# Latent attention in fp32 on one core: fixed places in the issue order for the probability splits, the output weights and the late loads

## The chip, the cores and the metric

The kernel runs on one of the eight cores of a Trainium2 chip. A core has a matrix engine (PE, whose weight loads are listed as PEld), a vector engine (DVE), an activation engine (ACT), a general engine (POOL), and a queue engine (SP) that issues most of the transfers. Each engine works through its own list of instructions in a fixed order, and waits on semaphores where it needs another engine's result. The metric is the device time of one execution in microseconds. Before the change it is 598.81 us, the median of three runs (596.79 to 600.26).

## The reference

The model has one layer that is used: an RMS norm, multi-head latent attention with a SiLU gate, an output projection, a residual add, and a last RMS norm. The sequence has 1024 positions, the width is 1024, there are 8 heads, everything is float32. Cut to what matters:

```
proj = rms_norm(x) @ w_in                     # c_q (384), c_kv (256), k_pe (64), gate (1024)
q = (rms_norm(c_q) @ w_uq)                    # 8 heads x (128 + 64 rotary)
k_nope, v = split(rms_norm(c_kv) @ w_ukv)     # 8 heads x (128, 128)
s = q_nope @ k_nope.T + rope(q_pe) @ rope(k_pe).T
p = softmax(s * scale)                        # per head, 1024 x 1024
o = (p @ v) * silu(gate)
y = rms_norm(x + o @ w_out)
```

## The kernel before

Float32 products are made of three products in a faster format: each operand is split into a high part and a low part (`hi` is a cast, `lo` is the operand less `hi`), and `mm3` issues high by high, high by low and low by high. So each operand of a product costs a cast, usually on ACT or POOL, and a subtraction, on DVE or POOL.

The program has three stages. In the first, up to about 175 us, the input projection, the gates, the norms and the rotary parts are made. In the second, 175 to 490 us, attention runs over 64 blocks: block u is head u // 8 and query rows (u % 8) * 128 to + 127. In the third the output projection runs over 8 row tiles and two column halves.

A block goes through this chain. `scores` (line 451) issues ten matmuls of 512 columns into a PSUM tile `s`; there are two such tiles, so block u + 2 can only start when block u has been read. DVE takes the row maxima (`nmx`, line 464). ACT takes the exponential into the tile `probs` with the row sums `sm` (line 466). DVE makes the reciprocal `rc` (line 471), POOL multiplies by it (line 472), and DVE transposes within 32 by 32 squares (line 473). Four blocks make a group g and share one `probs` tile, of which there are two. After the fourth, `exchange` (line 475) finishes the transpose across partitions by 16 transfers on SP from `probs` to a tile `d`. `split_part` (line 483) then splits one half of `d`, in two pieces c = 0 and 1: two casts `pt_h` on ACT (line 488), and the low parts `pt_l`, the first piece on DVE (line 490), the second half on DVE (line 492) and half on POOL (line 493). There are three buffers for the pieces. `values` (line 499) issues 12 matmuls for each half of a group, and after the second half DVE multiplies the result into `gate` (line 516). Beside that, each head makes its queries, keys and values from latent tensors (`q`, `k`, `v`), each with a cast on ACT and a subtraction on DVE.

In the last head the output weights are loaded on SP (`fetch_w_out`, line 523, four buffers `wor`) and split (`split_w_out`, line 527: a cast `woh` on ACT, a subtraction `wol` on DVE or POOL). `out_start` (line 547) loads a piece of x, splits the gated result of heads 0 to 6 into `o_split` (cast on ACT, subtraction on DVE) and issues 21 matmuls `o`; `out_end` adds head 7 and the residual.

The order in which the instructions of an engine stand is not the order in which the Python writes them. At build time a scheduler plays the program against its own expectation of durations and puts each instruction where that expectation has it ready, with the order of writing as priority (`later` moves a helper's priority back). The chip then follows that fixed order, whatever the real durations are. In the main loop (line 653) step u writes the scores of block u, and at even u the split of half `two` of group g, with u = 8 + 4 g + 2 two; at odd u the values of it.

Of the kernel before, what the change touches and what calls it, by code (L numbers as in the profile page):

```python
# [29 lines left out]
def kernel(  # L30
# [415 lines left out]
    produce_q(q_now, 0, w_q)  # L446
    produce_v(v_now, 0, w_v)

    square, part = {}, {}

    def scores(u, q, kx, qpe):
        half, qs = (u % 8) // 4, slice((u % 4) * P, (u % 4 + 1) * P)
        s = wide("s")
        qpe_s = qpe[half][:, qs]
        for kb in range(2):
            ks = halves(kb)
            mm3(s[:, ks], q[half][0][:, qs], q[half][1][:, qs], kx[kb][0], kx[kb][1], True, False)
            mm(s[:, ks], lhsT=qpe_s, rhs=kk_h[:, ks], start=False, stop=False)  # L458
            mm(s[:, ks], lhsT=qpe_s, rhs=kk_l[:, ks], start=False, stop=True)  # L459
        if u % 4 == 0:  # L460
            square[u // 4] = turned_tile("probs").rearrange("p j (k t c) -> p j k t c", k=8, t=4)
        p_t = square[u // 4][:, :, :, u % 4]
        nmx = column("nmx")
        nc.vector.tensor_reduce(nmx, s, axis=AX.X, op=ALU.max, negate=True)  # L464
        sm = column("sm")
        nc.scalar.activation(  # L466
            p_t.rearrange("p j k c -> p k j c"), s.rearrange("p (k j c) -> p k j c", k=8, j=4),
            AF.Exp, bias=nmx, accum_out=sm,
        )
        rc = column("rc")  # L470
        nc.vector.reciprocal(rc, sm)  # L471
        nc.gpsimd.tensor_scalar(p_t, p_t, rc, 1.0, op0=ALU.mult, op1=ALU.mult)  # L472
        nc.vector.transpose(out=p_t, in_=p_t)  # L473

    def exchange(g):

        src = square.pop(g).rearrange("p j k t c -> p j (k t c)")
        d = part[g] = at.tile([P, 4, L], F32, name="d", tag="d")
        for a in range(4):
            for j in range(4):  # L480
                nc.sync.dma_start(d[j * 32:(j + 1) * 32, a], src[a * 32:(a + 1) * 32, j])  # L481

    def split_part(g, two):

        for c in range(2):
            src = part[g][:, :, (two * 2 + c) * 256:(two * 2 + c + 1) * 256]
            hi, lo = split_tiles("pt")
            nc.scalar.copy(hi, src)  # L488
            if c == 0:
                nc.vector.tensor_sub(lo, src, f32(hi))  # L490
            else:
                nc.vector.tensor_sub(lo[:, 0:2], src[:, 0:2], f32(hi[:, 0:2]))  # L492
                nc.gpsimd.tensor_sub(lo[:, 2:4], src[:, 2:4], f32(hi[:, 2:4]))  # L493
            split_keys.append((hi, lo))
# [158 lines left out]
    for u in range(U + 10):  # L653
# [15 lines left out]
        if u % 2 == 0 and u >= 8:  # L669
            g, two = (u - 8) // 4, (u - 8) % 4 // 2  # L670
            if g < U // 4:
                split_part(g, two)
        if u % 2 == 1 and u >= 9:
            g, two = (u - 9) // 4, (u - 9) % 4 // 2
            if g < U // 4:
# [3 lines left out]
            split_w_out(H - 2, 0)  # L679
        if u == U + 1:  # L680
            split_w_out(H - 1, 0)
            for k in range(3):
                fetch_w_out(k, 1)
            y_sb = turned_tile("y_sb").rearrange("p a b -> p (a b)")
            gf_sb = wop.tile([P, D], F32, name="gf_sb")
            nc.sync.dma_start(gf_sb, gf)
            nc.gpsimd.tensor_scalar(gf_sb, gf_sb, -0.5, 1.0, op0=ALU.mult, op1=ALU.mult)
        if u in (U + 1, U + 3):
            started.append(out_start(0, len(started)))
        if u == U + 3:  # L690
            started.append(out_start(0, 2))
            out_end(started[0])
# [14 lines left out]
                produce_v(v_now, i - 3, w_v)  # L707
        if h == H - 1:
            if i >= 2:
                split_w_out(i - 2, 0)  # L710
            if i >= 1:
                fetch_w_out(i - 1, 0)
            continue
# [78 lines left out]
```

## Time and profile before

| what | us |
|---|---|
| median of three runs | 598.81 |
| the profiled execution | 599.52 |
| its span, first to last instruction | 597.7 |
| PE busy | 575.8 |
| DVE busy | 432.4 |
| ACT busy | 276.9 |
| POOL busy | 226.0 |
| mean granted PE clock, of 1 | 0.988 |

Three things help to read it. The end of a matmul is modelled: one of 512 columns is shown as 0.39 us long, while the next one starts 0.23 us after it, so PE is shown as busy even where it is only just kept fed, and its real lost time is found from the starts. The clock column says what share of full speed PE was granted: it falls after a pause. And a wait is put down to the last event that ended it; with engines that work in fixed order, what stands in front of an instruction matters as much as what it needs.

### The profile page before, as it was taken

The page shows a single profiled execution, that of the slowest core. Times are in us where ns is not written, and L with a number is a line of the kernel's source. Part 1 is how long each engine was busy: PE and PEld are TensorE (multiplying, and loading weights), DVE is VectorE, ACT ScalarE, POOL GpSimd, SP SyncE. Part 2 cuts the span into 40 slices and gives each one's busy share as a digit, 9 for nine tenths or more (in the row PEclk, how much of TensorE's full clock was granted, in tenths as well). Part 3 has the DMA queues.
Part 4 walks back from the last instruction along what each step waited for, and adds up shares of the span by engine and source line. Part 5 has one row for each costly group of instructions (what it writes and reads, how often), then busy time and mean ns, then how long its engine had stood idle before and what let it go on. Part 6 is the DMA issues. An engine that isn't in the chain of part 4 may idle for free.

```text
span 597.7 us, 7666 instructions
## 1 busy us (share of the span) xinstructions
PE 575.8 (96%) x2604; PEld 474.9 (79%) x2604; DVE 432.4 (72%) x578; ACT 276.9 (46%) x437; POOL 226.0 (38%) x197
## 2 busy tenths in 40 slices
PE   9999999999999999999999999999699979999995
PEld 6888888888888778877888778888588758888885
DVE  6912588565237899889898988988769995784653
ACT  4357553021024456526545444646346743554652
POOL 3513502343102353454344533455242664483000
PEclk9999999999999999999999999999889999999998
DMA  8666222233211646577617467353664886231342
GB/s 299 238 207 230 88 72 64 96 106 140 89 49 35 143 111 153 138 164 163 140 41 176 110 152 167 94 115 78 142 140 106 247 212 137 93 105 54 123 141 106
DMA packets 35963, 78.66 MB, mean 132 GB/s; under 512 B 7314, under 2 KB 11154, under 8 KB 35860
## 3 DMA queue, kind: packets, MB, share of 16 engines
q1 hardware_dynamic: 34628, 76.17, 47.0%
q10 hardware_dynamic: 1296, 2.01, 0.9%
q8 instruction: 20, 0.33, 0.2%
q14 instruction: 19, 0.16, 0.1%
HBM read 36.19 MB, written 8.41 MB: 75 GB/s over the span
## 4 chain that ended last, share of the span: by engine, by line
PE 64%; SPq 12%; DVE 8%; issue 7%; DMA 4%; ACT 3%; POOL 1%; POOLq 0%; ACTq 0%; DVEq 0%
SPq L481 12%; PE g L60 6%; PE g L59 6%; PE g L61 6%; PE o L61 5%; PE o L60 5%; PE o L59 5%; DVE probs L473 3%; PE pv L59 2%; PE pv L60 2%; PE pv L61 2%; PE s L59 2%; PE s L60 2%; PE s L458 2%; PE s L61 2%
## 5 line engine op out<-in xcount | busy, mean ns | idle before, releaser
L472 POOL TENSOR_SCALAR probs<-probs,rc 128x1024 f32<-128x1024 f32 x64 | 83.5, 1306 | 112.1 <-DVE rc L471 102.1
L466 ACT ACTIVATE probs<-s,nmx 128x1024 f32<-128x1024 f32 x64 | 71.4, 1116 | 99.8 <-DVE nmx L464 94.3
L473 DVE STREAM_TRANSPOSE probs<-probs 128x1024 f32<-128x1024 f32 x64 | 78.9, 1234 | 10.5 <-POOL probs L472 9.6
L464 DVE TENSOR_REDUCE nmx<-s 128x1 f32<-128x1024 f32 x64 | 76.8, 1208 | 9.9 <-PE s L459 9.7
L488 ACT CAST pt_h<-d 128x1024 fp32r<-128x1024 f32 x64 | 65.6, 1050 | 27.4 <-DMA d<-probs 13.4
L60 PE MATMUL g<-xl,gwh 128*128 128x512 f32 x160 | 62.3, 390 | 0.0
L61 PE MATMUL g<-xh,gwl 128*128 128x512 f32 x160 | 62.3, 389 | 0.0
L59 PE MATMUL g<-xh,gwh 128*128 128x512 f32 x160 | 62.3, 389 | 0.0
L493 POOL TENSOR_TENSOR pt_l<-d,pt_h 128x512 fp32r<-128x512 f32 x32 | 48.8, 1525 | 35.4 <-ACT pt_h L488 35.1
L59 PE MATMUL s<-k_h,q_h 128*128 128x512 f32 x128 | 50.4, 396 | 6.7 <-ACT probs L466 6.7
L59 PE MATMUL pv<-pt_h,v_h 128*128 128x512 f32 x128 | 50.5, 394 | 4.7 <-ACT pt_h L488 4.7
L490 DVE TENSOR_TENSOR pt_l<-d,pt_h 128x1024 fp32r<-128x1024 f32 x32 | 42.7, 1334 | 10.9 <-ACT pt_h L488 7.5
L60 PE MATMUL pv<-pt_l,v_h 128*128 128x512 f32 x128 | 50.1, 391 | 0.5 <-POOL pt_l L493 0.4
L60 PE MATMUL s<-k_l,q_h 128*128 128x512 f32 x128 | 50.0, 390 | 0.0
L458 PE MATMUL s<-kk_h,qpe 128*128 128x512 f32 x128 | 49.9, 390 | 0.0
L61 PE MATMUL s<-k_h,q_l 128*128 128x512 f32 x128 | 49.9, 390 | 0.0
L459 PE MATMUL s<-kk_l,qpe 128*128 128x512 f32 x128 | 49.9, 390 | 0.0
L61 PE MATMUL pv<-pt_h,v_l 128*128 128x512 f32 x128 | 49.9, 390 | 0.0
L61 PE MATMUL o<-woh,o_split 128*128 128x512 f32 (+1 forms) x118 | 45.1, 386 | 2.4 <-DVE o_split L576 2.4
L60 PE MATMUL o<-wol,o_split 128*128 128x512 f32 (+1 forms) x118 | 45.2, 383 | 0.0
L59 PE MATMUL o<-woh,o_split 128*128 128x512 f32 (+1 forms) x118 | 45.0, 383 | 0.0
L492 DVE TENSOR_TENSOR pt_l<-d,pt_h 128x512 fp32r<-128x512 f32 x32 | 32.9, 1029 | 4.7 <-ACT pt_h L488 4.7
(193 smaller groups left out, 1250.2 us busy)
## 6 DMA issues: line engine op xcount, KB each, us to landing
d<-probs SPq DMA_DIRECT2D x256, 128.0 KB
gwr<-in_wg SPq DMA_DIRECT2D x20, 256.0 KB
craw_b<-in_x SPq DMA_DIRECT2D x8, 512.0 KB
qpe<-qpe_d SPq DMA_DIRECT2D x16, 256.0 KB
wor<-in_wo SPq DMA_DIRECT2D x16, 256.0 KB
xr<-in_x SPq DMA_DIRECT2D x16, 256.0 KB
xr<-in_xT SPq DMA_DIRECT2D x5, 512.0 KB
qpe_d<-craw_a SPq DMA_DIRECT2D x8, 256.0 KB
```

What stands on the lines that cost most here:

```text
L59: mm(ps, lhsT=lh, rhs=rh, start=first, stop=False)
L60: mm(ps, lhsT=lh, rhs=rl, start=False, stop=False)
L61: mm(ps, lhsT=ll, rhs=rh, start=False, stop=last)
L458: mm(s[:, ks], lhsT=qpe_s, rhs=kk_h[:, ks], start=False, stop=False)
L459: mm(s[:, ks], lhsT=qpe_s, rhs=kk_l[:, ks], start=False, stop=True)
L464: nc.vector.tensor_reduce(nmx, s, axis=AX.X, op=ALU.max, negate=True)
L466: nc.scalar.activation(p_t.rearrange("p j k c -> p k j c"), s.rearrange("p (k j c) -> p k j c", k=8, j=4), AF.Exp, bias=nmx, accum_out=sm,)
L472: nc.gpsimd.tensor_scalar(p_t, p_t, rc, 1.0, op0=ALU.mult, op1=ALU.mult)
L473: nc.vector.transpose(out=p_t, in_=p_t)
L481: nc.sync.dma_start(d[j * 32:(j + 1) * 32, a], src[a * 32:(a + 1) * 32, j])
L488: nc.scalar.copy(hi, src)
L493: nc.gpsimd.tensor_sub(lo[:, 2:4], src[:, 2:4], f32(hi[:, 2:4]))
```

## The change

`tc.issue_after(ins)` adds an edge of order to each instruction written in its block, on the engine of `ins`: it stands behind `ins` in that engine's list. It adds no semaphore. The change keeps each block's exponential in `exps[u]` and the last transfer of each exchange in `moves[g]`, and uses them in five places:

- the split of a half group, written at step u, has its casts on ACT behind the exponential of block u - 1 (the split of group g, first half, behind block 4 g + 7; second half behind block 4 g + 9);
- in the last head the split of output weight i - 2, written at step u, has its cast behind the exponential of block u - 1;
- the load of the last norm's gain `gf` and the first three loads of the second half of the output weights stand on SP behind the last transfer of the last exchange;
- the first two `out_start` have their casts on ACT behind the last exponential, and their loads of x on SP behind the last exchange;
- the weight loads are written after the load of `gf`, no longer before it.

No operation is added or removed. Since the scheduler plays the program again with these edges, the order on all engines moves after the first few blocks.

```diff
-    square, part = {}, {}
+    square, part, exps, moves = {}, {}, {}, {}
...
-        nc.scalar.activation(
+        exps[u] = nc.scalar.activation(
             p_t.rearrange("p j k c -> p k j c"), s.rearrange("p (k j c) -> p k j c", k=8, j=4),
             AF.Exp, bias=nmx, accum_out=sm,
         )
...
-                nc.sync.dma_start(d[j * 32:(j + 1) * 32, a], src[a * 32:(a + 1) * 32, j])
+                moves[g] = nc.sync.dma_start(d[j * 32:(j + 1) * 32, a], src[a * 32:(a + 1) * 32, j])
...
             if g < U // 4:
-                split_part(g, two)
+                with tc.issue_after(exps[min(u, U) - 1].ins):
+                    split_part(g, two)
...
             split_w_out(H - 1, 0)
-            for k in range(3):
-                fetch_w_out(k, 1)
             y_sb = turned_tile("y_sb").rearrange("p a b -> p (a b)")
             gf_sb = wop.tile([P, D], F32, name="gf_sb")
-            nc.sync.dma_start(gf_sb, gf)
+            with tc.issue_after(moves[U // 4 - 1].ins):
+                nc.sync.dma_start(gf_sb, gf)
+                for k in range(3):
+                    fetch_w_out(k, 1)
             nc.gpsimd.tensor_scalar(gf_sb, gf_sb, -0.5, 1.0, op0=ALU.mult, op1=ALU.mult)
         if u in (U + 1, U + 3):
-            started.append(out_start(0, len(started)))
+            with tc.issue_after(exps[U - 1].ins), tc.issue_after(moves[U // 4 - 1].ins):
+                started.append(out_start(0, len(started)))
...
             if i >= 2:
-                split_w_out(i - 2, 0)
+                with tc.issue_after(exps[u - 1].ins):
+                    split_w_out(i - 2, 0)
```

Three places show what it does to the lists. The first is ACT around blocks 46 to 51 (head 5 into head 6). `probs_3433` is the tile of group 11 (blocks 44 to 47), `probs_3610` that of group 12; `d_3381` is the exchanged group 10, `d_3569` group 11. Before:

```order
L466 ACTIVATE probs_3433,sm_3510<-s_3497,nmx_3508 128x8x4x32
L488 CAST pt_h_3619<-d_3381 128x1024
L488 CAST pt_h_3623<-d_3381 128x1024
L466 ACTIVATE probs_3433,sm_3538<-s_3525,nmx_3536 128x8x4x32
...
L466 ACTIVATE probs_3610,sm_3693<-s_3680,nmx_3691 128x8x4x32
L488 CAST pt_h_3790<-d_3569 128x1024
L488 CAST pt_h_3794<-d_3569 128x1024
L466 ACTIVATE probs_3610,sm_3721<-s_3708,nmx_3719 128x8x4x32
```

And now:

```order
L466 ACTIVATE probs_3433,sm_3510<-s_3497,nmx_3508 128x8x4x32
L466 ACTIVATE probs_3433,sm_3538<-s_3525,nmx_3536 128x8x4x32
L488 CAST pt_h_3619<-d_3381 128x1024
L488 CAST pt_h_3623<-d_3381 128x1024
...
L466 ACTIVATE probs_3610,sm_3693<-s_3680,nmx_3691 128x8x4x32
L466 ACTIVATE probs_3610,sm_3721<-s_3708,nmx_3719 128x8x4x32
L488 CAST pt_h_3790<-d_3569 128x1024
L488 CAST pt_h_3794<-d_3569 128x1024
```

The casts of an exchanged group, which wait for its transfers, stood in front of the exponentials of blocks 47 and 51 and now stand behind them. The same holds for both casts of groups 2, 5 and 6, and for one of the two casts of groups 9, 12 and 13.

The second is DVE in the same group, for blocks 44 and 45 (`nmx_3434`, `nmx_3462`). Before, and with it the first row of block 46:

```order
L464 TENSOR_REDUCE nmx_3434<-s_3422 128x1
L464 TENSOR_REDUCE nmx_3462<-s_3451 128x1
L471 RECIPROCAL rc_3438<-sm_3436 128x1
L431 SCALAR_TENSOR_TENSOR q_l_3494<-q_3483,q_h_3493 128x512
L65 TENSOR_TENSOR wk_l_3564<-wk_r_3565,wk_h_3563 128x256
L471 RECIPROCAL rc_3466<-sm_3464 128x1
L473 STREAM_TRANSPOSE probs_3433<-probs_3433 128x32x32
L492 TENSOR_TENSOR pt_l_3521<-d_3193,pt_h_3520 128x512
```

And now:

```order
L464 TENSOR_REDUCE nmx_3434<-s_3422 128x1
L464 TENSOR_REDUCE nmx_3462<-s_3451 128x1
L471 RECIPROCAL rc_3438<-sm_3436 128x1
L471 RECIPROCAL rc_3466<-sm_3464 128x1
L473 STREAM_TRANSPOSE probs_3433<-probs_3433 128x32x32
L490 TENSOR_TENSOR pt_l_3517<-d_3193,pt_h_3516 128x1024
```

Two maxima are followed at once by two reciprocals, where two subtractions stood between the reciprocals before. Ten pairs of blocks from block 18 on have that form now.

The third is ACT at the end of attention: blocks 60 to 63 (`probs_4186`), the splits of groups 13 (`d_3939`) and 14 (`d_4139`), the output weights (`woh0` to `woh6`) and the first splits of the gated result (`o_split`). Before:

```order
L466 ACTIVATE probs_4014,sm_4133<-s_4120,nmx_4131 128x8x4x32
L543 CAST woh1_4169<-wor1_0_4118 128x512
L488 CAST pt_h_4199<-d_3939 128x1024
L543 CAST woh2_4204<-wor2_0_4173 128x512
L488 CAST pt_h_4267<-d_3939 128x1024
L543 CAST woh3_4242<-wor3_0_4208 128x512
L575 CAST o_split_4383<-gate_363 128x384
L575 CAST o_split_4437<-gate_363 128x384
L466 ACTIVATE probs_4186,sm_4189<-s_4175,nmx_4187 128x8x4x32
...
L575 CAST o_split_4467<-gate_363 128x512
L466 ACTIVATE probs_4186,sm_4295<-s_4282,nmx_4293 128x8x4x32
L488 CAST pt_h_4337<-d_4139 128x1024
```

And now:

```order
L466 ACTIVATE probs_4014,sm_4133<-s_4120,nmx_4131 128x8x4x32
...
L543 CAST woh1_4169<-wor1_0_4118 128x512
L543 CAST woh2_4204<-wor2_0_4173 128x512
L488 CAST pt_h_4199<-d_3939 128x1024
L543 CAST woh6_4348<-wor6_0_4335 128x512
L466 ACTIVATE probs_4186,sm_4189<-s_4175,nmx_4187 128x8x4x32
...
L466 ACTIVATE probs_4186,sm_4295<-s_4282,nmx_4293 128x8x4x32
L575 CAST o_split_4381<-gate_363 128x512
...
L575 CAST o_split_4467<-gate_363 128x512
L488 CAST pt_h_4337<-d_4139 128x1024
```

The casts of `o_split` moved from ahead of the last exponentials to behind the last one, where five of them stand in a row. The cast of output weight 6, which stood behind all exponentials, now stands in front of that of block 60, and on SP its load moved ahead of the exchange of group 14. Weight 6 has no edge of its own; the scheduler put it there.

## The prediction

> **What bounds the kernel now.** I read the page first, for the engines and the groups.
>
> ```profile
> PE 575.8 (96%) x2604; PEld 474.9 (79%) x2604; DVE 432.4 (72%) x578; ACT 276.9 (46%) x437; POOL 226.0 (38%) x197
> L472 POOL TENSOR_SCALAR probs<-probs,rc 128x1024 f32<-128x1024 f32 x64 | 83.5, 1306 | 112.1 <-DVE rc L471 102.1
> L473 DVE STREAM_TRANSPOSE probs<-probs 128x1024 f32<-128x1024 f32 x64 | 78.9, 1234 | 10.5 <-POOL probs L472 9.6
> L488 ACT CAST pt_h<-d 128x1024 fp32r<-128x1024 f32 x64 | 65.6, 1050 | 27.4 <-DMA d<-probs 13.4
> L490 DVE TENSOR_TENSOR pt_l<-d,pt_h 128x1024 fp32r<-128x1024 f32 x32 | 42.7, 1334 | 10.9 <-ACT pt_h L488 7.5
> L492 DVE TENSOR_TENSOR pt_l<-d,pt_h 128x512 fp32r<-128x512 f32 x32 | 32.9, 1029 | 4.7 <-ACT pt_h L488 4.7
> ```
>
> PE is the bound, so only time in which PE stands still can be won: the rest of the matmuls stays. The PE timeline gives the places, from which I take those behind block 10, where the lists begin to differ (two small stops ahead of it stay as they are). The number in brackets is the idle time, counted from the modelled end of the matmul before.
>
> ```profile
> 204.94 0.39 PE L59 MATMUL s<-k_h,q_h 128*128 128x512 f32 x1
> 206.98 0.39 PE L459 MATMUL s<-kk_l,qpe 128*128 128x512 f32 x1
> ...
> 266.06 0.50 PE L59 MATMUL s<-k_h,q_h 128*128 128x512 f32 x1 [0.35 <-ACT probs L466]
> 270.15 0.50 PE L59 MATMUL s<-k_h,q_h 128*128 128x512 f32 x1 [1.53 <-ACT probs L466]
> ...
> 341.84 0.50 PE L59 MATMUL s<-k_h,q_h 128*128 128x512 f32 x1 [0.75 <-ACT probs L466]
> 348.07 0.50 PE L59 MATMUL s<-k_h,q_h 128*128 128x512 f32 x1 [1.41 <-ACT probs L466]
> ...
> 430.52 0.80 PE L59 MATMUL pv<-pt_h,v_h 128*128 128x512 f32 x1 [4.70 <-ACT pt_h L488]
> 431.11 0.63 PE L59 MATMUL q<-cq_h,wq_h 128*128 128x512 f32 x1
> 434.52 0.63 PE L61 MATMUL q<-cq_h,wq_l 128*128 128x512 f32 x1
> ...
> 478.04 0.50 PE L60 MATMUL pv<-pt_l,v_h 128*128 128x512 f32 x1 [0.40 <-POOL pt_l L493]
> 484.77 0.50 PE L59 MATMUL s<-k_h,q_h 128*128 128x512 f32 x1 [1.43 <-ACT probs L466]
> 491.32 0.79 PE L61 MATMUL o<-woh,o_split 128*128 128x512 f32 x1 [2.39 <-DVE o_split L576]
> 491.92 0.63 PE L59 MATMUL o<-woh,o_split 128*128 128x512 f32 x1
> 494.05 0.60 PE L61 MATMUL o<-woh,o_split 128*128 128x512 f32 x1
> ```
>
> From 204.94 to 206.98 nine matmuls start, 0.227 apart. A matmul is shown 0.39 long, so a bracket leaves out 0.16; the first matmul after a pause is 0.11 longer (0.50). So a stop costs its bracket plus 0.27. After the two longest the pitch is (434.52 - 431.11) / 8 = 0.426 and (494.05 - 491.92) / 5 = 0.426, nearly twice the usual: 2.0 us more for the ten matmuls behind 430.52, 1.4 for the seven behind 491.32. Two lots follow: **middle** (266 to 431) 8.74 + 5 x 0.27 + 2.0 = 12.1; **end** (478 to 494) 4.22 + 0.81 + 1.4 = 6.4.
>
> What makes the middle? The ACT and SP timelines show it.
>
> ```profile
> 246.40 2.96 ACT L488 CAST pt_h<-d 128x1024 fp32r<-128x1024 f32 x3 [2.21 <-DMA d<-probs]
> 268.89 1.11 ACT L466 ACTIVATE probs<-s,nmx 128x1024 f32<-128x1024 f32 x1 [2.89 <-DMA d<-probs]
> ...
> 326.03 2.00 ACT L488 CAST pt_h<-d 128x1024 fp32r<-128x1024 f32 x2 [1.65 <-DMA d<-probs]
> ...
> 406.02 2.00 ACT L488 CAST pt_h<-d 128x1024 fp32r<-128x1024 f32 x2 [2.13 <-DMA d<-probs]
> 407.93 1.10 ACT L466 ACTIVATE probs<-s,nmx 128x1024 f32<-128x1024 f32 x1
> ...
> 415.95 11.38 SPq L481 DMA_DIRECT2D d<-probs  x16
> 421.84 0.19 ACT L466 ACTIVATION_READ_ACCUMULATOR probs<-s,nmx 128x1 f32 x1
> 429.42 1.99 ACT L488 CAST pt_h<-d 128x1024 fp32r<-128x1024 f32 x2 [7.39 <-DMA d<-probs]
> 431.32 1.11 ACT L466 ACTIVATE probs<-s,nmx 128x1024 f32<-128x1024 f32 x1
> ```
>
> The four casts here are the whole 13.4 us that line 488 waits for transfers. The first three are groups 2, 6 and 10, each in front of the exponential of the next group's last block (15, 31, 47). That block is then late, so its group's exchange is: for block 47 the exponential waits until 407.93 and the exchange is issued from 415.95 to 427.33, lands at 429.4, and there the casts of group 11 stand in front of block 51, and PE before the values of group 11. The same chain 160 us earlier ends at 268.89: block 20 writes the tile that the late exchange of group 3 still reads. So one wrong place in ACT's list makes each of the three clusters, 80 us apart.
>
> **The change part by part.**
>
> Splits behind a later exponential: the first two of ACT's orders shown above. Nothing is added, and the casts keep their 1.05 us. Their exponential no longer waits for a transfer. What is late next: the casts themselves. From the last transpose of a group the exchange takes 10.1 (16 issues) + 2.47 (landing, in the chain of waits), and the transpose ends some 5 us after its exponential (reciprocal, 1.31, 1.23 and DVE's queue): 17.6 in all.
>
> ```profile
> 426.73 2.47 DMA d<-probs
> 360.00:400.00 40.00, 40.00 (x189) 33.63 (x188) 35.69 (x44) 20.89 (x31) 19.19 (x16) 1.00 0.50 116
> ```
>
> Four blocks are 40 + 24 + 15 matmuls (scores, values, q and k), 17.9 us, and 19.4 with their share of v. So the exchange lands about when block 4 g + 7 ends, or 1 to 2 us before, and a wait there would meet an ACT that has nothing else for some 3 us. I count the whole middle, -12.1; the smallest that the mechanism allows is the stop at 430 alone, 4.97 + 2.0 = -7.0, the largest -12.1, since no more is lost there.
>
> The new pairs on DVE: in the stretch 360 to 400, without a PE stop, DVE is busy 35.69 of 40. A pair of blocks lasts 9.7 us of PE on average (half of 19.4), so DVE has 1.05 us to spare in each. Two reciprocals in a row make DVE wait for the second exponential, 1.12 and its read of the sums 0.19 after the maximum, 1.3 us, with nothing ahead of it to do. That is 0.25 to 0.3 over, in ten pairs: +2.8. Below, 0: DVE may fall behind some 2 to 3 us before PE notices, since PE has 12 to 24 other matmuls (2.7 to 5.4 us) between pairs of scores. Above, 1.0 in each of ten pairs (pairs without v last 8.95 us, leaving 0.2 to 0.3): +10. I take +2.8, nearer the free end, because the heavier pairs lend time to the lighter.
>
> The Trainium skill (GPSIMD Engine Reference, section "Key points") says that POOL and DVE contend for their memory interface when a DVE instruction has two SBUF inputs. The groups above agree: line 490 takes 1.33 for a whole piece, and line 492 takes 1.03 for half a one, beside which POOL works on the other half. By that rule alone the new list, which often puts DVE's half later than POOL's, would make DVE shorter by up to 1.03 - 0.67 = 0.36 in such a pair, and the sum better by up to 3.6 in the ten.
>
> The end. I walk it from the start of block 58's scores at 0, with DVE 2 us behind, by these rows and those above.
>
> ```profile
> 425.24 2.31 DVE L464 TENSOR_REDUCE nmx<-s 128x1 f32<-128x1024 f32 x2
> ...
> 467.11 3.16 DMA wor<-in_wo
> ...
> 469.85 0.62 ACT L543 CAST woh<-wor 128x512 fp32r<-128x512 f32 x1
> 470.55 1.30 POOL L544 TENSOR_TENSOR wol<-wor,woh 128x512 fp32r<-128x512 f32 x1 [0.69 <-ACT woh L543]
> 487.01 1.13 ACT L575 CAST o_split<-gate 128x512 fp32r<-128x512 f32 x2
> 497.04 10.05 SPq L481 DMA_DIRECT2D d<-probs  x16
> ...
> L586 DVE TENSOR_TENSOR y_sb<-o,xr x8: 673/686/693, 521.2 to 547.5; 128x512 f32<-128x512 f32 x8
> ```
>
> The maxima of 58 and 59 take 4.5 to 6.8, the exponential of 58 ends at 6.9, weight 0's cast at 7.5, the exponential of block 59 at 8.7; a cast of 1.05 and those of weights 1 and 2 end at 11; POOL has weight 2's low part at 12.3 and DVE weight 1's at 12.4; only then are two buffers free, SP issues loads 5 and 6 by 13.5, load 6 lands at 16.7, its cast ends at 17.3. Block 60's exponential, behind it, ends at 18.6. PE wants to start block 62 at 15.65 and stands 3.0. Then block 63's maxima come at 25.5 to 26.6, its exponential ends at 27.9, the first `o_split` is on DVE at 29.8: PE, out of values at 25.9, stands 4.0. The values of group 14 follow after only two `o` matmuls, behind five casts of 0.57 and one of 1.05, at 31.6: 1.2 more. With three restarts, and the clock for about five matmuls of 0.2, this makes 9.4 against 6.4: +3.0. The lists free something too: DVE has up to five subtractions of `o_split` less ahead of block 63's work. If that decides, the end gains 2 (-2). If the load lands later, or POOL's scaling of `gf` (now between two `pt_l` and behind a load issued after 10 us of exchange) holds the last values by 2, it loses 7 (+7).
>
> SP: `gf`, three weight loads and three of x go behind the last exchange. Their users come late (the first residual sum is at 521, and the exchange before ended its issue at 507), so 0, except POOL's `gf` above. Three more weight loads ahead of group 14's exchange: that exchange waits for block 59's transpose anyway, near 13.6 in the walk.
>
> Sum: -12.1 + 2.8 + 3.0 = -6.3. The profiled execution, 597.7 of span with 1.8 around it, becomes 593.2; it was 0.7 above the median, so I forecast 598.81 - 6.3 = **592.5**.
>
> **The clock.** Behind 2.39 idle the clock fell as it did behind 4.70; behind 1.53 it did not. The Trainium skill (TensorE: Matmul & The Clock Gate, Part 1: The HAM clock gate) puts the fall at an idle window of about 3.4 us. The trace's 2.39 speaks against it as a fixed length. By that rule only the 4.0 us stop in the walk would cost clock, which is what I have counted.
>
> **The rivals.**
>
> *DVE takes over.* All of the ten pairs cost 1.0, so 10 in place of 2.8: 599.7, no change. For: 35.69 of 40 busy, and a pair has less to fill a wait with. Against: in the list before, DVE kept up from 348 to 425 without a stop of PE.
>
> *The change moves the wait and doesn't remove it.* The exchange lands after block 4 g + 7, so ACT stands there as before, now in front of block 4 g + 8, and half of the middle stays: -6.1 + 5.8 = -0.3, 598.5. For: the margin above is 0.3 to 1.8 us. Against: the three late exchanges come from late exponentials, which now go first.
>
> *The values wait (slower).* Each half group's casts come behind an exponential that itself follows DVE; then `pt_l` follows on a full DVE. I find about 2 us between the last `pt_l` and the matmul that needs it. From the point where DVE is over 2 us further behind, every half group stops PE: 0.9 us in each of 24 between blocks 10 and 58 is 21.6, in place of the 2.8: -12.1 + 21.6 + 3.0 = +12.5, 611.3. For: PE reads these pieces in a fixed place. Against: while PE stands, DVE catches up, so the stops can't all be that long.
>
> **How the numbers follow.** I give the forecast 0.60, with its own range from 587 to 597; DVE taking over 0.16; the moved wait 0.12; the values waiting 0.12. A change under 0.5%, 3 us, can't be told from none here. Faster (under 595.8): nine tenths of the forecast, 0.54, and a third of the two middle rivals, 0.09: 0.63. Slower (over 601.8): the slower rival and a quarter of DVE taking over, 0.15. Same: 0.22. The range for 8 in 10 takes the forecast with the least loss at the end and no DVE wait, 598.81 - 14.1 = 584.7, about 585, and on the other side the two middle rivals with a little over, 601.
>
> **What would show it.** Right: no cast on line 488 waiting over 1 us for a transfer in front of a block that is ready; the exchanges of groups 3, 7 and 11 issued 3 us or more sooner after their block's scores; no PE stop over 1 us between 240 and 460. For the DVE term: idle time of DVE before line 471 of 10 us or more in all. For the end: a cast of weight 6 that waits for a load, and a stop before the first `o` near 4 us. I am wrong if the middle keeps its stops, or if they come back in front of `pv`.

## The result, and the profile after

The changed kernel takes 590.56 us, the median of four runs (589.25 to 590.82), against 598.04 for the kernel before (four runs, 596.79 to 600.26). The ratio is 0.9866, with a 95% interval of 0.9831 to 0.9901. The forecast was 592.5. The profiled execution took 590.82, with a span of 589.0, where the one before had 599.52 and 597.7. So 8.7 us went between the two traces.

The page of the changed kernel has these engine totals and groups:

```profile
PE 572.9 (97%) x2604; PEld 473.3 (80%) x2604; DVE 423.3 (72%) x578; ACT 274.6 (47%) x437; POOL 225.1 (38%) x197
L488 ACT CAST pt_h<-d 128x1024 fp32r<-128x1024 f32 x64 | 65.4, 1053 | 8.5 <-PE pv L61 5.2
```

The casts on line 488 waited 27.4 before, 13.4 of it for transfers into `d`. Now they wait 8.5, and a transfer is no longer what they wait for most. The waits of ACT in the stretch from 200 to 460, the longest sums first (total, times, longest one), have no entry that names `d<-probs` on line 488. The exponential waits for DVE's maxima, and line 488's longest sum names a weight's transfer:

```profile
ACT probs L466 <- DVE nmx L464: 104.8, 31, 5.7
...
ACT pt_h L488 <- DMA wk_r<-in_wuk: 2.9, 1, 2.9
```

The name misleads here. This one wait is that of the first-half casts of group 1, as the timeline of ACT shows:

```profile
230.42 2.00 ACT L488 CAST pt_h<-d 128x1024 fp32r<-128x1024 f32 x2 [2.86 <-DMA wk_r<-in_wuk]
```

They read `d` and nothing of that weight. SP had issued the last transfer of group 1's exchange by 228.12, and the weight's load followed at 228.22. So what they waited for is most likely their exchange. In the kernel before, the same casts waited 1.61 at 230.51, under the same name.

The exchanges of groups 3, 7 and 11, from the timeline of the DMA queue, start 7 to 11 us earlier in the span than before, where the last of them was issued at 415.95:

```profile
249.72 10.16 SPq L481 DMA_DIRECT2D d<-probs  x16
...
328.65 10.98 SPq L481 DMA_DIRECT2D d<-probs  x16
...
404.76 11.35 SPq L481 DMA_DIRECT2D d<-probs  x16
```

PE's own waits from 231 to the end of the span are four in number. Before, they were eight, 13.0 us in all:

```profile
PE o L59 <- ACT o_split L575: 4.4, 1, 4.4
PE s L59 <- ACT probs L466: 1.6, 1, 1.6
PE pv L60 <- DVE pt_l L492: 0.5, 1, 0.5
PE pv L59 <- ACT pt_h L488: 0.2, 1, 0.2
```

The PE timeline says where they are, and the rows behind each say what the clock did. Between 231.52 and 464.94 there is no stop.

```profile
464.94 0.47 PE L60 MATMUL pv<-pt_l,v_h 128*128 128x512 f32 x1 [0.47 <-DVE pt_l L492]
...
467.93 0.61 PE L59 MATMUL s<-k_h,q_h 128*128 128x512 f32 x1 [1.60 <-ACT probs L466]
468.34 0.63 PE L60 MATMUL s<-k_l,q_h 128*128 128x512 f32 x1
...
482.20 0.79 PE L59 MATMUL o<-woh,o_split 128*128 128x512 f32 x1 [4.39 <-ACT o_split L575]
482.79 0.63 PE L60 MATMUL o<-wol,o_split 128*128 128x512 f32 x1
```

The starts of matmuls give the account. I cut it at the first scores of block 0 and of block 58, because the same number of matmuls lies between the two in both kernels. The first part went from 283.1 to 270.2 us, which is 12.9 won. The second, from block 58 to the last matmul, went from 128.0 to 132.5, which is 4.5 lost. Together 8.4 of the 8.7. Below, the first part is called the middle and the second the end; in the changed kernel they are 270.2 and 132.5.

### The profile page after: what moved, and what is told of

Its sections match the earlier page's. It is cut to its first block, busy times and chain, and to the rows that moved or that the text cites. A ratio compares the mean times of both kernels' runs of the same rounds, so it can differ in the third digit from the quotient of the medians.

```text
span 589.0 us, 7656 instructions
## 1 busy us (share of the span) xinstructions
PE 572.9 (97%) x2604; PEld 473.3 (80%) x2604; DVE 423.3 (72%) x578; ACT 274.6 (47%) x437; POOL 225.1 (38%) x197
## 4 chain that ended last, share of the span: by engine, by line
PE 87%; SPq 3%; DVE 3%; DMA 2%; ACT 2%; issue 1%; POOL 0%; POOLq 0%; ACTq 0%; DVEq 0%
PE g L61 6%; PE g L60 6%; PE g L59 6%; PE o L59 5%; PE o L60 5%; PE o L61 5%; PE pv L59 4%; PE pv L60 4%; PE pv L61 4%; PE s L59 4%; PE s L61 4%; PE s L60 4%; PE s L458 4%; PE s L459 4%; SPq L481 3%; PE q L59 2%
## 5 line engine op out<-in xcount | busy, mean ns | idle before, releaser
L472 POOL TENSOR_SCALAR probs<-probs,rc 128x1024 f32<-128x1024 f32 x64 | 84.8, 1326 | 114.8 <-DVE rc L471 113.5
L490 DVE TENSOR_TENSOR pt_l<-d,pt_h 128x1024 fp32r<-128x1024 f32 x32 | 46.2, 1445 | 3.3 <-DMA xr<-in_x 1.8
L576 DVE TENSOR_TENSOR o_split<-gate,o_split 128x512 fp32r<-128x512 f32 (+2 forms) x48 | 30.9, 676 | 10.7 <-ACT o_split L575 10.7
## 6 DMA issues: line engine op xcount, KB each, us to landing
d<-probs SPq DMA_DIRECT2D x256, 128.0 KB
```

## The experiments

**Only the split edge.** The kernel before, with one of the five edges of order:

```diff
-        nc.scalar.activation(
+        exps[u] = nc.scalar.activation(
...
-                split_part(g, two)
+                with tc.issue_after(exps[min(u, U) - 1].ins):
+                    split_part(g, two)
```

> The kernel before with one edge alone: the casts of each half group behind the later exponential. Up to block 53 ACT's list is then that of the changed kernel, at the end it is close to that of before. Theory M (the three clusters of stops at 266 to 431 come from casts that wait for transfers in front of the exponentials of blocks 15, 31, 47 and 51; the other edges only lose time at the end): the middle's 12 to 13 us are won and the end stays, 598.0 - 12.5 = 585.5, between 584 and 588, so faster than the changed kernel's 590.56. Rival E (the edges on output weights and late loads bring a share of the gain): 590 to 594.

It took 589.85 (588.43 to 592.82), ratio 0.9853 (0.9829 to 0.9877). That is above the 584 to 588 of theory M and next to the range of rival E, so the time alone doesn't settle it; the stretches do. The middle is 270.2, the same as with all five. So the whole gain comes from the split edge. But the end did not stay: it is 130.3, or 130.7 if two matmuls that moved ahead of block 58 are counted to it. So part of the loss comes with the split edge too, in five small stops of PE between 465 and 480 and two later ones.

**Everything but the split edge.** The changed kernel, with that edge undone:

```diff
-                with tc.issue_after(exps[min(u, U) - 1].ins):
-                    split_part(g, two)
+                split_part(g, two)
```

> The changed kernel without the edge on the casts of the half groups; all other edges stay. Up to block 53 ACT's list is that of before. Theory M: all three clusters are back, ACT line 488 waits 13 us for transfers again; the end has the first splits of the gated result behind the last exponential but weight 6 no longer ahead of block 60, so it loses 1 to 3 against before: 599 to 601. Rival E: the other edges win by themselves, 592 to 596.

It took 600.36 (597.70 to 602.69), ratio 1.0026 (1.0007 to 1.0044). The middle is back at 282.9, with all five stops in their old places, as the PE timeline shows:

```profile
265.98 0.50 PE L59 MATMUL s<-k_h,q_h 128*128 128x512 f32 x1 [0.35 <-ACT probs L466]
270.21 0.50 PE L59 MATMUL s<-k_h,q_h 128*128 128x512 f32 x1 [1.63 <-ACT probs L466]
...
342.19 0.50 PE L59 MATMUL s<-k_h,q_h 128*128 128x512 f32 x1 [1.06 <-ACT probs L466]
348.44 0.50 PE L59 MATMUL s<-k_h,q_h 128*128 128x512 f32 x1 [1.40 <-ACT probs L466]
...
431.06 0.80 PE L59 MATMUL pv<-pt_h,v_h 128*128 128x512 f32 x1 [4.83 <-ACT pt_h L488]
```

The other four edges lost 1.8 at the end (129.8 against 128.0) and won nothing.

**Only three pairs of casts.** The claim behind the middle was that the first-half casts of groups 2, 6 and 10 make each cluster, and that those of groups 3, 7 and 11 only pass the delay on. So the edge was put on those three half groups alone:

```diff
-                split_part(g, two)
+                if two == 0 and g in (2, 6, 10):
+                    with tc.issue_after(exps[u - 1].ins):
+                        split_part(g, two)
+                else:
+                    split_part(g, two)
```

> The kernel before, with the order edge only on the first half splits of groups 2, 6 and 10, whose casts stood in front of the exponentials of blocks 15, 31 and 47; every other split, the weights and the late loads are written as before. Theory (one misplaced pair of casts makes each of the three clusters of stops): all five stops between 266 and 431 go, the stretch from the first scores to block 58 falls from 283.1 to 269 to 272, and with the end as in the split alone the time is 587 to 592. Rival (each cluster has causes of its own, since groups 3, 7 and 11 also have casts in front of blocks 19, 35 and 51): the stops at 270, 348 and 431 stay, the stretch is 276 to 281 and the time 594 to 599.

One run: 592.83. Of the five stops one is left, as the PE timeline shows, and a new one of 0.25 stands 2.4 us before it:

```profile
342.59 0.50 PE L59 MATMUL s<-k_h,q_h 128*128 128x512 f32 x1 [0.92 <-ACT probs L466]
```

The middle is 269.8, but here ten matmuls (nine of `q` and one of `pv`, 2.3 us) have moved behind block 58, so it compares as 272.1: 11.0 of the 12.9 come from three pairs of casts. The end, without those ten matmuls, is 132.2, so this small edit lost 4.2 there, nearly as much as the whole change did. The time is 0.8 above what the theory gave, because I had given it the milder end of the split edge.

**How much more DVE could carry.** The middle leaves DVE with idle time in front of reciprocals, and I had priced it as loss. Here DVE gets one more maximum for each of blocks 10 to 55, over 256 or over 512 columns, whose result nothing uses:

```diff
         nmx = column("nmx")
+        if 10 <= u < 56:
+            nc.vector.tensor_reduce(g_sb[:, 0:1], s[:, 0:256], axis=AX.X, op=ALU.max)
         nc.vector.tensor_reduce(nmx, s, axis=AX.X, op=ALU.max, negate=True)
```

> The changed kernel, with one more maximum on DVE over 256 columns of the scores ahead of the row maxima of blocks 10 to 55; its result is used by nothing. An estimate from the 1.15 of 1024 columns is 0.35 a block, 15 us more DVE work, and DVE goes from 184 of 210 busy to 199. Elastic (DVE may be late by some us, and its waits shrink as it falls behind): the stretch from block 10 to block 58 stays within 232.9 and 236, the time 590 to 594. Rigid (in a pair of blocks 1.05 us is to spare, of which 0.7 goes, while waits of 0.8 to 1.3 us in front of a reciprocal can't be filled): 0.5 to 0.9 for each of 23 pairs, the stretch 244 to 254, the time 602 to 612.

> The same with 512 columns: an estimate of 0.65 a block, 30 us in all, so that DVE's work in 210 us would be 212. Elastic: DVE is the bound by a little, the stretch from block 10 to block 58 grows by 3 to 12 us to 236 to 245, the time 594 to 603. Rigid: 1.1 to 1.6 a pair of blocks, 25 to 37 us, the time 616 to 628.

They took 594.5 and 598.49, one run each. The groups by line give what was really added, 18.5 and 30.8 us, of the kernel with 256 and then of the one with 512 columns:

```profile
L464 DVE TENSOR_REDUCE g_sb<-s 128x1 f32<-128x256 f32 x46 | 18.5, 402 | 0.3 <-PE s L459 0.3
```

```profile
L464 DVE TENSOR_REDUCE g_sb<-s 128x1 f32<-128x512 f32 x46 | 30.8, 670 | 1.4 <-PE s L459 1.4
```

From block 10 to block 58 they needed 236.7 and 243.5, where the changed kernel needs 232.9. So 18.5 us of extra work cost 3.7, and 30.8 cost 10.6, or 9.5 without five matmuls that moved into that stretch. The first is 0.7 above the elastic theory's bound, the second inside it, and the rigid theory's 244 for the first and 258 for the second (25 us more than 232.9) were not reached. The table of the stretch from 240 to 450 (PE, PEld, DVE, ACT, POOL busy) shows DVE filling up from 184.07 of 210 to 194.07 and 202.56, for the changed kernel, 256 and 512 columns:

```profile
240.00:450.00 210.00, 210.00 (x995) 176.66 (x994) 184.07 (x231) 109.07 (x166) 96.62 (x78) 1.00 0.56 131
```

```profile
240.00:450.00 210.00, 207.25 (x979) 173.42 (x978) 194.07 (x270) 108.03 (x162) 93.45 (x76) 1.00 0.58 133
```

```profile
240.00:450.00 210.00, 204.44 (x943) 167.50 (x942) 202.56 (x266) 107.28 (x158) 87.01 (x75) 1.00 0.58 133
```

In the same stretch DVE's waits in front of the reciprocal fell from 10.0 us to 6.6 and to 1.9, and those for POOL in front of the transpose from 10.1 to 1.5 and 1.1. This would follow if DVE gets later and finds its inputs there when it comes. But the test has a limit: the scheduler saw the extra work and laid out DVE's list anew, so that of the ten pairs of reciprocals only one is left in each kernel. So the waits may also have shrunk by the new order. The test shows how much slack DVE has, not what one such pair costs.

**Weight 6 back behind the last exponential.** My account of the end began with the cast of weight 6, which waits for its load in front of block 60's exponential:

```diff
-            split_w_out(H - 2, 0)
+            with tc.issue_after(exps[U - 1].ins):
+                split_w_out(H - 2, 0)
```

> The changed kernel with one more edge: the cast of output weight 6 behind the last exponential too. Theory W (the cast that waits 4.35 us for its load in front of block 60's exponential makes the 1.6 us stop before block 62 and the half clock behind it, and delays block 63): 1.8 + 1.7 us of stop and clock are won, 0.6 of cast is added in front of the first split of the gated result: 587 to 588.5. Rival D (at the end DVE is late anyway, and the stop moves to the first output product): 589.5 to 591.

It took 589.89 (589.15 to 590.41), ratio 0.9847 (0.9829 to 0.9865). The wait for the load is gone and the end is 131.0, so this cast was worth 1.5 of the 4.5, by one trace of each kernel; the medians are only 0.7 apart, and their intervals overlap. The stop before the first `o` did not shrink, as the rival had it:

```profile
466.88 0.50 PE L59 MATMUL s<-k_h,q_h 128*128 128x512 f32 x1 [0.75 <-ACT probs L466]
...
480.42 0.80 PE L59 MATMUL o<-woh,o_split 128*128 128x512 f32 x1 [4.92 <-ACT o_split L575]
```

**And the first splits of the gated result free again.** The same, and the first two `out_start` no longer behind the last exponential:

```diff
-            with tc.issue_after(exps[U - 1].ins), tc.issue_after(moves[U // 4 - 1].ins):
+            with tc.issue_after(moves[U // 4 - 1].ins):
```

> The changed kernel with weight 6 behind the last exponential and without the edge that puts the first splits of the gated result behind it; the scheduler places these splits between the exponentials of blocks 59 to 63, as before the change. Theory W: the 4.4 us stop before the first output product shrinks to about the 2.4 of before and the one before block 62 goes: the end is as before the change, 585 to 587. Rival D (these splits' subtractions on a full DVE delay the last maxima by as much as they save): as e3, 587 to 589.

It took 591.04 (590.00 to 591.99), ratio 0.9868 (0.9847 to 0.9888), with an end of 133.2; that is slower than both the theory and the rival gave. ACT again has the first of those casts ahead of the last exponentials. Their low parts stand on DVE among the last maxima and reciprocals, and PE stops six times in place of three, four of them for DVE's `pt_l` and `o_split`. So putting these casts early in ACT's list does not shorten the end; the stops are then for DVE.

**Less work for DVE there.** The kernel with weight 6 behind, and the low parts of the output weights all on POOL in the first half:

```diff
-        (nc.vector if k % 2 else nc.gpsimd).tensor_sub(wl, wr, f32(wh))
+        (nc.vector if k % 2 and nh else nc.gpsimd).tensor_sub(wl, wr, f32(wh))
```

> The changed kernel, with weight 6 split behind the last exponential, and with all low parts of the first half of the output weights on POOL, where DVE made every other one. Theory (DVE is late at the end, so what is taken off it ahead of block 63 comes back on PE): two to three subtractions of 0.66 to 1.2 us less, the stretch from block 58 to the last matmul falls from 131.0 to 128 to 129.5 and the time is 587 to 588.7. Rival (POOL, which scales the probabilities of the last blocks, is delayed as much by three more subtractions of 1.30): the same 589.5 to 591.5 as with weight 6 alone.

It took 589.11 (587.97 to 589.93), ratio 0.9831 (0.9806 to 0.9857), end 130.5. This can't be told from the 589.89 without it: the intervals overlap for the most part. The same edit on the kernel with the split edge alone:

> The kernel before with the split edge alone, and all low parts of the first half of the output weights on POOL. With the split alone the end lost 2.3 us against before, in five small stops of which two name DVE. Theory (DVE late at the end): the stretch from block 58 to the last matmul falls from 130.3 to 128 to 129.5, time 587.5 to 589. Rival (the small stops come from ACT's list, where casts of weights and of o_split stand ahead of the last exponentials): the same 589 to 591.

589.21 (588.78 to 589.71), ratio 0.9844 (0.9826 to 0.9863), end 130.3 as without it. So these few subtractions are not what hurts at the end. (The rival for this kernel, that its small stops come from ACT's list, was not tested by itself.)

**The last maxima first.** If not the amount, the order. The DVE timeline of the kernel before this one (weight 6 behind, low parts on POOL) shows the last maxima, the second row of line 464, where they stand:

```profile
470.83 1.22 DVE L464 TENSOR_REDUCE nmx<-s 128x1 f32<-128x1024 f32 x1
471.97 1.75 DVE L492 TENSOR_TENSOR pt_l<-d,pt_h 128x512 fp32r<-128x512 f32 x1
473.64 1.23 DVE L473 STREAM_TRANSPOSE probs<-probs 128x1024 f32<-128x1024 f32 x1
474.80 1.18 DVE L464 TENSOR_REDUCE nmx<-s 128x1 f32<-128x1024 f32 x1
```

The scores of block 63 were done at 471.96. The maxima stood 2.8 us longer behind a subtraction and a transpose. Both are put behind them:

```diff
-        nc.vector.tensor_reduce(nmx, s, axis=AX.X, op=ALU.max, negate=True)
+        maxima[u] = nc.vector.tensor_reduce(nmx, s, axis=AX.X, op=ALU.max, negate=True)
+        if u == U - 1:
+            with tc.issue_after(maxima[u].ins):
+                for work in held:
+                    work()
...
-        nc.vector.transpose(out=p_t, in_=p_t)
+        if u == U - 3:
+            held.append(lambda: nc.vector.transpose(out=p_t, in_=p_t))
+        else:
+            nc.vector.transpose(out=p_t, in_=p_t)
...
-                    split_part(g, two)
+                    split_part(g, two, (0, 1) if u != U - 2 else (0,))
+        if u == U - 1:
+            with tc.issue_after(exps[U - 3].ins), tc.issue_after(maxima[U - 1].ins):
+                split_part(13, 1, (1,))
```

> The kernel with weight 6 behind the last exponential and all first-half low parts on POOL, and in addition on DVE the transpose of block 61 and the low parts of the last piece of group 13 behind the row maxima of block 63. In that kernel those maxima could have started 2.4 us after block 63's scores did, and started 5.3 after, behind such a subtraction and such a transpose. Theory (the stop of 4.39 before the first o is the last maxima standing in DVE's list): the maxima start under 3.5 us after the scores of block 63, the first o comes 7 to 8.5 us after them instead of 10.1, the values of group 13 stop PE by up to 2 us instead, and of the stretch of 130.4 from block 58 to the last matmul 1.5 to 3 go: 586.5 to 588. Rival (the end is bound by the last exchange, its splits and POOL, and PE has enough else to do before it): the stop goes and comes back in front of the last values or the o behind them, stretch 130 to 131, time 588.5 to 590.

It took 586.76 (586.35 to 587.31), ratio 0.9806 (0.9787 to 0.9824), end 128.3. The stop before the first `o` went from 4.39 to 0.83, and 1.59 came up in front of the values of group 13, as the theory had it. (That product reads `pt_l`, whose subtraction on DVE ended at 474.60; the view names the reciprocal that followed it.) But part of the rival showed too. The transposes of blocks 62 and 63 now stood behind three and five subtractions of `o_split`, the last exchange was issued at 483.81, where the kernel without this edit had it at 480.85, and the last values stopped twice:

```profile
474.74 0.47 PE L60 MATMUL pv<-pt_l,v_h 128*128 128x512 f32 x1 [1.59 <-DVE rc L475]
476.97 0.50 PE L59 MATMUL o<-woh,o_split 128*128 128x512 f32 x1 [0.83 <-ACT o_split L582]
...
498.43 0.50 PE L60 MATMUL pv<-pt_l,v_h 128*128 128x512 f32 x1 [0.70 <-DVE pt_l L497]
501.01 0.50 PE L60 MATMUL pv<-pt_l,v_h 128*128 128x512 f32 x1 [0.93 <-POOL pt_l L500]
```

**And the last transposes.** So the second `out_start` gives way to the transpose of block 63 (`flips[u]` keeps the transposes):

```diff
             with tc.issue_after(exps[U - 1].ins), tc.issue_after(moves[U // 4 - 1].ins):
-                started.append(out_start(0, len(started)))
+                with tc.issue_after(flips[U - 1].ins if started else exps[U - 1].ins):
+                    started.append(out_start(0, len(started)))
```

> The kernel with the last maxima first, and in addition on DVE the second piece of the gated result's split (out_start of row tile 1) behind the transpose of block 63. In the kernel with the last maxima first, three subtractions of o_split and a wait stood ahead of the transposes of blocks 62 and 63, the last exchange was issued at 483.81 instead of 480.85 of the run before it, and the values of group 15 stopped PE by 0.70 and 0.93. Theory (the last exchange is now what is late): it is issued 2 to 3.3 us sooner, both stops go, 1.6 plus twice 0.27 make 2.1: stretch from block 58 to the last matmul 126 to 127.3, time 584.5 to 586. Rival (ACT's and POOL's splits of groups 14 and 15 are late for themselves, or the matmuls of o stop for the splits that are now later): the exchange comes sooner and the stretch stays at 128 to 129, time 586.2 to 588.

It took 584.76 (584.33 to 585.33), ratio 0.9773 (0.9749 to 0.9797): the best of all, with an end of 126.4, which is 1.6 shorter than in the kernel before the change. The exchange is issued at 480.79 and both late stops are gone. The waits of PE from 231 on:

```profile
PE pv L60 <- DVE rc L475: 1.6, 1, 1.6
PE pv L60 <- DVE nmx L464: 1.1, 1, 1.1
PE o L59 <- ACT o_split L582: 0.8, 1, 0.8
...
```

The first two are again products that read `pt_l`, and no reciprocal or maximum.

**The late loads free.** The changed kernel without its order on SP:

```diff
-            with tc.issue_after(moves[U // 4 - 1].ins):
-                nc.sync.dma_start(gf_sb, gf)
-                for k in range(3):
-                    fetch_w_out(k, 1)
+            nc.sync.dma_start(gf_sb, gf)
+            for k in range(3):
+                fetch_w_out(k, 1)
...
-            with tc.issue_after(exps[U - 1].ins), tc.issue_after(moves[U // 4 - 1].ins):
+            with tc.issue_after(exps[U - 1].ins):
```

> The changed kernel without the order of SP's late loads: gf, three weight loads and the first x loads are no longer behind the last exchange. My term for them is 0: the same stops at the end, the stretch from block 58 to the last matmul 132 to 133, time 589 to 592. Rival (POOL's scaling of gf, behind a load that now comes 10 us later, or the later weights hold the end): the stretch falls by 1 to 2, time 588 to 589.5; or the loads delay the last exchange by their issue time of 0.5 to 2.5 and the stretch grows by that.

One run: 591.99, end 134.0 against 132.5. The rival of a shorter end falls, and the other one, that the loads get in the way, fits. The DMA queue's timeline shows the loads of `gf` and x at 455.02, ahead of the three weight loads that take until 464.52:

```profile
455.02 0.43 SPq L685 DMA_DIRECT2D gf_sb<-in_gf  x1
455.50 2.23 SPq L551 DMA_DIRECT2D xr<-in_x  x3
457.93 6.59 SPq L525 DMA_DIRECT2D wor<-in_wo  x3
```

Weight 6 is among them; its cast ends at 467.87, which is 18.5 after block 58's start, 1.5 later than in the changed kernel. And POOL scales `gf` at 461.42, ahead of a weight's low part and of the half piece that PE waits for at 465.44:

```profile
461.42 1.05 POOL L688 TENSOR_SCALAR gf_sb<-gf_sb 128x1024 f32<-128x1024 f32 x1 [2.40 <-DMA gf_sb<-in_gf]
462.43 1.74 POOL L544 TENSOR_TENSOR wol<-wor,woh 128x512 fp32r<-128x512 f32 x1
464.12 1.26 POOL L493 TENSOR_TENSOR pt_l<-d,pt_h 128x512 fp32r<-128x512 f32 x1
```

PE stopped 1.39 there, where it had stopped 0.47, and 2.16 in place of 1.60 before block 62. So the order on SP seems to win about 1.5 us, though one run can't give that an interval, and it was tried only with weight 6's cast in front of block 60's exponential.

## Why the prediction was right, and where its terms were off

The forecast was right in sign and by 2 us in size. Against the profiled execution it had -6.3, and -8.7 was measured. Its mechanism for the middle was right; that the total came so near is partly luck, since the DVE term was 2.8 too high and the end 1.5 too low. (The chances for slower add up to 0.16, not 0.15.)

**The middle, -12.1: measured -12.9.** The mechanism held. Undoing the split edge brought the five stops back, and the edge alone took them away; on three pairs of casts it took away four of the five. Of the signs that I had named, one came in full: no stop of PE lies between 240 and 460. One came with an exception: the casts of group 1 still wait 2.86, most likely for their exchange, in front of block 12, whose maxima were ready at 228.87 and whose exponential started at 232.32. They stood there before too, and PE waited 0.20 for them. A third was only partly there. From the start of a group's last scores to the issue of its exchange it took 15.2, 14.1 and 14.8 us before for groups 3, 7 and 11, and 9.6, 11.8 and 10.6 now: 5.5, 2.3 and 4.1 sooner, one of them under the 3 that I had asked for. The rival in which the wait moves in front of block 4 g + 8 fell with that: block 12 is the only place of that kind, and in the middle's three clusters the margin I had put at 0.3 to 1.8 us was enough.

**The new pairs on DVE, +2.8: measured 0.** This is the step that failed. The wait itself came as described. DVE's groups by line, with the idle time before each, have 15.3 us for the exponential in front of the reciprocal, where it was 4.6:

```profile
L490 DVE TENSOR_TENSOR pt_l<-d,pt_h 128x1024 fp32r<-128x1024 f32 x32 | 46.2, 1445 | 3.3 <-DMA xr<-in_x 1.8 <-DMA qpe<-qpe_d 0.7 <-ACT pt_h L488 0.4
L492 DVE TENSOR_TENSOR pt_l<-d,pt_h 128x512 fp32r<-128x512 f32 x32 | 24.9, 779 | 1.5 <-ACT pt_h L488 1.4
L471 DVE RECIPROCAL rc<-sm 128x1 f32<-128x1 f32 x64 | 9.7, 152 | 17.4 <-ACT probs L466 15.3
```

In eight of the ten pairs the two maxima stand right ahead of the reciprocals; seven of these waited 1.1 where I had 1.3, and the last 2.6. In the other two a subtraction stands between, and they waited 0.5 and 0.6. And PE never stopped for it: I charged each pair with what its wait exceeded its own spare time by, as if nothing could be carried from one pair to the next. The bound of 0 that I had written down, with PE holding 2.7 to 5.4 us of other matmuls, was the right end. The extra maxima fit that: DVE took 18.5 us more work for 3.7 us of time. That the waits of a pair vanish as DVE falls behind is argued and not shown, since those runs had a new order with one pair left. The rival in which DVE takes over, and the slower one in which every half group's values wait, fell by the same trace: behind block 10 the view has two waits of PE for `pt_h` or `pt_l`, 0.2 and 0.47 us.

The two subtractions changed too. Line 492 fell from 1.03 to 0.78 on the mean and line 490 rose from 1.33 to 1.45, so their sum went from 75.6 to 71.1 us. POOL was busy for half of the time or more beside 22 of the 32 subtractions of line 492 before, and beside 11 now; for line 490 it was 15, and 21 now. The Trainium skill (GPSIMD Engine Reference, "Key points") says that DVE and POOL contend when a DVE instruction has two SBUF inputs; the direction agrees with this trace. No time of PE can be put down to it here, since DVE had slack anyway.

**The end, +3.0: measured +4.5.** The stops that the walk named were there: 3.0 before block 62 became 0.47 and 1.60, 4.0 before the first `o` became 4.39, and the 1.2 in front of group 14's values did not come. The clock was mis-sized most: I gave it 1.0, and twice a half clock cost about 1.6 behind 467.93 and 1.4 behind 482.20 (seven or eight matmuls, 0.2 each). With 0.27 for each of three restarts this is 10.3 against the 9.4 of the walk, where 6.4 was before. The remaining 0.6 of the 4.5 are two short stops that carry no bracket: two products of the values of group 13 start at 474.62 and 476.42, which is 0.42 and 0.53 behind the matmul ahead of each in place of 0.23, and with their restarts this makes 0.7. The walk's own sum was also off: stops of 3.0, 4.0 and 1.2, three restarts of 0.27 and 1.0 of clock make 10.0 and not 9.4, so +3.6, and a forecast of 593.1.

And the cause I named covers a third of it. Weight 6's cast did wait for its load, as predicted, and ended at 466.77, 17.0 after block 58's start (the walk had 17.3). Putting it right returned 1.5. The longest stop that is left, before the first `o`, follows DVE's order, which the walk had too early: it had the last maxima end at 26.6, but they ended at 28.7 (478.54), behind a subtraction of 1.78 and a transpose of 1.23 that the walk does not name. They started 3.0 after the end of their scores, where it was 1.7 before the change. The first `o` came at 32.4 in place of 29.8. Moving DVE's work away did nothing that can be measured; putting the maxima first won 2.4 us, and the transposes 2.0 more. So this order can win back more than the 3.0 that were left. That it is also what lost them is argued and not shown: the other edits on the casts lost something at the end too, 2.7 with the split edge alone, 1.8 without it and 4.2 with three pairs.

**SP, 0: -1.5 by one run.** This is a share of the end's +4.5, which would have been larger without it. I had looked only at who uses the late loads, and not at what they stood in front of. Freed, they go ahead of weight loads, and `gf`'s scaling goes ahead of POOL's splits. In the changed kernel that scaling waited 12.2 us for its load, as the bound of +7 had feared, and no engine waited for it.

## What to carry to other kernels

A cast that waits for a transfer holds everything behind it on its engine, and with shared buffers one such place shows as stops of another engine 16 to 25 us later; find the first, and put ready work ahead of it. Idle time on an engine that runs just ahead of the bound may be slack and not loss: load it on purpose before you price its waits. Where a pipeline drains, look at which of the ready instructions the busy helper engine takes first (here the maxima of the last block, then the transposes that the last exchange needs), and not only at how much it has to do.

## What the runs showed that was not expected

**The clock's fall does not follow from the length of a stop alone.** In the changed kernel PE's pitch, from one start to the next, went to 0.43 behind a stop of 1.60, with one of 0.47 three us ahead of it. In the kernel with 256 more columns on DVE a stop of 1.60, with one of 0.82 three us ahead, left the pitch at 0.23:

```profile
471.76 0.50 PE L59 MATMUL s<-k_h,q_h 128*128 128x512 f32 x1 [1.60 <-ACT probs L468]
472.09 0.40 PE L60 MATMUL s<-k_l,q_h 128*128 128x512 f32 x1
```

In the kernel with the first splits free again the pitch rose to 0.42 only from the fourth matmul behind a stop of 2.03, as its PE timeline shows:

```profile
469.33 0.50 PE L59 MATMUL s<-k_h,q_h 128*128 128x512 f32 x1 [2.03 <-ACT probs L466]
469.67 0.39 PE L60 MATMUL s<-k_l,q_h 128*128 128x512 f32 x1
469.90 0.45 PE L61 MATMUL s<-k_h,q_l 128*128 128x512 f32 x1
470.15 0.63 PE L458 MATMUL s<-kk_h,qpe 128*128 128x512 f32 x1
```

Stops of 1.41 to 1.63 with no other in the four us ahead never cost clock, and stops of 4.38 and more always did. Why 1.60 cost clock once and not the other time, no run here settles.

The Trainium skill (TensorE: Matmul & The Clock Gate, "Part 1: The HAM clock gate") puts the fall behind an idle window of about 3.4 us and says that this window runs freely and does not start anew with a kernel. The late fall and the two outcomes for 1.60 agree with a free-running window. That the window has to be idle throughout does not agree: 1.60, 2.03 and 2.39 are all shorter.

**The same subtraction on DVE takes 0.64 to 1.78 us.** Line 492's durations in the changed kernel (shortest, median and longest, in ns), and DVE's timeline ahead of the last maxima:

```profile
L492 DVE TENSOR_TENSOR pt_l<-d,pt_h x32: 641/678/1784, 214.1 to 509.1; 128x512 fp32r<-128x512 f32 x32
```

```profile
474.49 1.78 DVE L492 TENSOR_TENSOR pt_l<-d,pt_h 128x512 fp32r<-128x512 f32 x1
476.19 1.23 DVE L473 STREAM_TRANSPOSE probs<-probs 128x1024 f32<-128x1024 f32 x1
477.36 1.18 DVE L464 TENSOR_REDUCE nmx<-s 128x1 f32<-128x1024 f32 x1
```

Three of them took 1.78. One of the three stands just there, while POOL subtracted from 472.21 to 475.72. A walk that takes the median for such a place is 1.1 us too early.
